# Weight splits in half-tile buffers with a longer lookahead, in an fp32 encoder trunk

## The chip, the cores and the metric

The kernel runs on one core of a Trainium2 chip. The metric is the time of one execution on the device, in microseconds, as the median of several runs. The core has five engines that work side by side, each through its own instructions in order: TensorE (PE: matmuls, and transposes as matmuls with the identity), VectorE (DVE), ScalarE (ACT), GpSimd (POOL) and SyncE (SP, which here issues loads). They wait for one another through semaphores. SBUF is the memory on the core, PSUM holds the results of matmuls in eight banks.

## The reference, cut to what matters

Two layers, 256 tokens of width 1024, everything in float32. Each layer is

```
x = x + 1/2 * SwiGLU_1(RMSNorm(x))                 # width 2816
h = RMSNorm(x)
[qA kA vA qB kB vB] = h @ W_in
oA = windowed attention (8 query heads, 2 key heads, distance bias, sink logit)
oB = differential attention (4 heads, two softmaxes), RMSNorm per head
x = x + concat(oA, oB) @ W_out
x = x + 1/2 * SwiGLU_2(RMSNorm(x))
```

with `SwiGLU(h) = (silu(h @ w_gate) * (h @ w_up)) @ w_down`, and a last RMSNorm. So there are four SwiGLU blocks, called mixers here, and two attention parts.

## The kernel before, in words

**Split operands.** PE multiplies in a float32 form of fewer bits (`float32r`). Each operand is therefore split in two: `hi` is the operand cast to that form, `lo` is the operand minus `hi`, and a product is the sum of three matmuls, hi·hi, lo·hi and hi·lo (`tokens`, lines 474 to 483; `narrow`, line 495; `prod`, line 569). Weights are split after they are loaded: ACT casts `raw` to `whi`, DVE subtracts and writes `wlo` (`emit_split`, lines 167 to 190).

**Weight tiles.** All weights are consumed in one fixed order, a list of `Step`s (`specs`, line 100 and lines 226 to 268), most of them 512 input rows by 512 columns, 1 MB. `emit_dma` (line 154) issues a load into one of six `raw` buffers, `emit_split` splits it into one of three `whi` and one of three `wlo` buffers. `weights()` (line 219) hands out the next tile i, and before that calls `ahead(i + 2)` (line 198), which emits the splits up to tile i + 2 and loads beyond it. A buffer of tile i - 1 is taken by tile i + 2, so the cast of tile i + 2 waits until PE has done its last matmul with tile i - 1. Each tile is split in two cuts of 1024 columns in all, or in four of 512 (tiles 0 to 3 and those of the attention part).

**A mixer** (`ffn`, lines 547 to 679) takes the 2816 hidden columns in five groups of 512 and a last one of 256. Group 0 uses tiles 0 to 3, group 1 tiles 4 to 9: four tiles of gate and up weights (24 matmuls each), and two of the down weights for the group before. After the first tile of a group PE transposes the hidden tile of the group before (`turn`, line 618), ACT casts it and DVE makes its `lo` part (`split`, line 485). Groups 2 and 4 (`SEVEN`, line 31) are computed by a scheme with seven products of half the size in place of eight (`by_seven`, lines 579 to 616; tiles 10 to 18 in group 2): of weights and inputs some are sums, which `make_sums` (line 304) makes on DVE during group 1 for the inputs, and for the weights `seven` (line 115) makes by DVE additions (`raw += raw`) and by loads that add into a raw buffer, issued by POOL. The order in `by_seven`: product 1 (tile 10), product 2 (tile 11), `turn` of the hidden tile, product 3 (tile 12), the first down tile (13), products 4 to 7 (tiles 14 to 17), the second down tile (18).

**Attention** (`mix`, line 723): four narrow projections, scores of four head pairs of each kind, softmax on DVE and ACT, transposes of the probabilities, products with the values, the output projection. In the first part of it the engines' order is that of the text; between `kept[0] = False` (line 796) and `kept[0] = True` (line 897) a scheduler orders the instructions of each engine. Everywhere else instructions stay in the order in which the program emits them, so a cast that waits for its buffer holds up what stands behind it on ACT, and its subtraction what stands behind it on DVE.

Tiles named `s4` (16 blocks of 4 KB per partition) hold the normed inputs, the hidden tiles, the input sums, softmax results and others; `q` (three blocks) and `v` (one) are used by attention alone.

Of the kernel before, what the change touches and what calls it, by code (L numbers as in the profile page):

```python
# [10 lines left out]
F32R = mybir.dt.float32r  # L11
AF = mybir.ActivationFunctionType
ALU = mybir.AluOpType
# [21 lines left out]
def trunk(ctx: ExitStack, tc: tile.TileContext, x, n1, g1, u1, d1, nm, w_in, sink,  # L35
# [128 lines left out]
        if s.behind is not None:  # L164
            s.behind()

    def emit_split(i):
        s = specs[i]
        kn, n, raw = s.kn, s.n, raws[s.src]
        hi = wp.tile([P, kn, n], F32R, tag="whi", bufs=N_HI, name=nm_("whi"))  # L170
        lo = wp.tile([P, kn, n], F32R, tag="wlo", bufs=N_LO, name=nm_("wlo"))
        loaded[i] = (hi, lo)
        cuts = [0, kn // 2, kn] if i > 1 and (i not in fine or kn < 4) else [kn * j // 4 for j in range(5)]
        for a, b in zip(cuts, cuts[1:]):
            if n == D:
                views = [(t[0][:, a:b, c:c + 512], t[1][:, a:b, c:c + 512], t[2][:, a:b, c:c + 512])
                         for t in [(raw, hi, lo)] for c in (0, 512)]
            elif i not in paired:
                views = [(raw[:, a:b], hi[:, a:b], lo[:, a:b])]
            else:  # L180
                views = [(raw.rearrange("p k (s c d) -> p c k s d", s=2, c=2)[:, c, a:b],
                          hi.rearrange("p k (c s d) -> p c k s d", s=2, c=2)[:, c, a:b],
                          lo.rearrange("p k (c s d) -> p c k s d", s=2, c=2)[:, c, a:b]) for c in range(2)]
            for r_, h_, l_ in views:
                act.copy(h_, r_)
                dve.tensor_tensor(l_, r_, f(h_), op=ALU.subtract)
            if i < 2:
                yield
        for k in s.free:
            raws.pop(k)  # L190

    def emit_early(i):
        yield from emit_dma(i)
        yield from emit_split(i)

    at = dict(use=0, dma=2, prep=2, split=2)

    def ahead(n):

        n = min(n, len(specs) - 1)  # L200
        while True:
            if at["split"] <= n and at["prep"] > at["split"]:
                for _ in emit_split(at["split"]):
                    pass
                at["split"] += 1
            elif at["prep"] <= min(n + 1, len(specs) - 1) and at["dma"] > at["prep"] and \
                    (specs[at["prep"]].prep is None or at["split"] >= at["prep"]):
# [65 lines left out]
    class Norm:  # L273
# [115 lines left out]
    def take_x(k):  # L389
# [8 lines left out]
        elif k == 1:  # L398
            for e in (g, u, g, u):
                next(e)  # L400
            norm.pair(2)
            ahead(2)
            norm.pair(3)
        elif k == 2:
            ahead(3)
# [65 lines left out]
            dve.tensor_scalar_mul(gsub[:, l:l + 1], gcol[:, 48 + l:49 + l], 1.0 - lam_init[l])  # L471


    def tokens(accs, xs, w, k0, ks=range(4), first=0, last=KC - 1, order=None):

        hi, lo = w
        for k, t in (order or [(k, t) for k in ks for t in range(2)]):
            kk = k0 + k
            xv = xs[kk // 2][:, kk % 2]
            xh, xl = xv[:, t * P:(t + 1) * P], xv[:, S + t * P:S + (t + 1) * P]  # L480
            pe.matmul(accs[t], lhsT=xh, rhs=hi[:, k], start=kk == first, stop=False)
            pe.matmul(accs[t], lhsT=xl, rhs=hi[:, k], start=False, stop=False)
            pe.matmul(accs[t], lhsT=xh, rhs=lo[:, k], start=False, stop=kk == (last if isinstance(last, int) else last[t]))

    def split(dst, src, scale=None):

# [7 lines left out]

    def narrow(acc, w, j, xs, kcs, first, last):

        hi, lo = w
        for i, (wk, xk) in enumerate(kcs):
            wh = hi[:, wk, j * P:(j + 1) * P]
            wl = lo[:, wk, j * P:(j + 1) * P]  # L500
# [46 lines left out]
    def ffn(norm, aside=None, before=None, final=False):  # L547
# [19 lines left out]
            return h  # L567

        def prod(xo, w):
            hi, lo = w  # L570
            acc = bank()
            for k in range(4):
                xh, xl = xo(k)
                pe.matmul(acc, lhsT=xh, rhs=hi[:, k], start=k == 0, stop=False)
                pe.matmul(acc, lhsT=xl, rhs=hi[:, k], start=False, stop=False)
                pe.matmul(acc, lhsT=xh, rhs=lo[:, k], start=False, stop=k == 3)
            return acc

        def by_seven(h, g):
# [104 lines left out]
    def ffn_end(parts, last):  # L684
# [4 lines left out]
        w = {0: weights()}  # L689

        def group(h, order, a=None, c=slice(None), first=0):
            tokens(a or accs[h], hT, [t[:, :, c] for t in w[h]], G4, first=first, last=last[h], order=order)

        def tail(h, order=BY_TOKENS, a=None, c=slice(None)):
            tokens(a or accs[h], [None] * (2 * NGRP) + hE, [t[:, h, :, c] for t in w["rest"]], 4 * NGRP, last=last[h], order=order)
# [4 lines left out]
        w["rest"] = [t.rearrange("p k (h n) -> p h k n", h=2) for t in weights()]  # L700
        w[1] = weights(LOOK - 1)
        return group, tail

    def ffn_close(parts, nxt):
# [18 lines left out]
    def mix(l, norm, nxt_norm):  # L723
# [111 lines left out]
        vB = tp.tile([P, 2, 512], F32, tag="v", bufs=1, name=nm_("v"))  # L835
        vsl = [bank() for _ in range(2)]
        for k0 in (0, 4):
            hi, lo = weights()
            for k in range(4):
                kk = k0 + k  # L840
                xv = norm.xs[kk // 2][:, kk % 2]
                for t in range(2):
                    xh, xl = xv[:, t * P:(t + 1) * P], xv[:, S + t * P:S + (t + 1) * P]
                    pe.matmul(vsl[t], lhsT=xh, rhs=hi[:, k], start=kk == 0, stop=False)
                    pe.matmul(vsl[t], lhsT=xl, rhs=hi[:, k], start=False, stop=False)
                    pe.matmul(vsl[t], lhsT=xh, rhs=lo[:, k], start=False, stop=kk == KC - 1)
# [73 lines left out]
        res = Residual(nxt_norm, accs)  # L920

        def out_part(w, k0, h, order=None):
            tokens(accs[h], oT, [t.rearrange("p k (h n) -> p h k n", h=2)[:, h] for t in w], k0, range(2), 4, 3, order)

        w = weights()
        for h in range(2):
# [112 lines left out]
```

## Time and profile before

| | before |
|---|---|
| median of 3 runs | 945.48 us (945.32 to 945.58) |
| profiled execution | 945.94 us |
| its span, first to last instruction | 944.2 us |
| DVE busy, ACT busy | 718.6 us, 538.1 us |
| PE matmuls ps<-whi,s | 699.4 us in 2252 rows |
| PE matmuls ps<-wlo,s | 438.1 us in 1126 rows |
| DVE subtractions into wlo | 433.8 us in 440 |
| ACT casts into whi | 372.0 us in 440 |
| DMA | 186.19 MB, mean 197 GB/s |
| granted TensorE clock | 0.999 |

A row of the profile names the engine, the operation, what it writes and reads by the program's names, the shapes, and how many instructions it stands for; behind a bar, or in brackets, stands the idle time of the engine just ahead of it and what ended that. All program lines show as L50, since every instruction passes one helper, so rows are told apart by their tiles: `whi` and `wlo` are split weights, `s` the s4 tiles, `tmp` and `ps` scratch and PSUM. Matmuls overlap: a row of PE lasts longer than the time until the next one may start. In the timeline the first column is the start in us from the start of the span, the second the time from the first start to the last end.

### The profile page before, as it was taken

The page shows a single profiled execution, that of the slowest core. Times are in us where ns is not written, and L with a number is a line of the kernel's source. Part 1 is how long each engine was busy: PE and PEld are TensorE (multiplying, and loading weights), DVE is VectorE, ACT ScalarE, POOL GpSimd, SP SyncE. Part 2 cuts the span into 40 slices and gives each one's busy share as a digit, 9 for nine tenths or more (in the row PEclk, how much of TensorE's full clock was granted, in tenths as well). Part 3 has the DMA queues.
Part 4 walks back from the last instruction along what each step waited for, and adds up shares of the span by engine and source line. Part 5 has one row for each costly group of instructions (what it writes and reads, how often), then busy time and mean ns, then how long its engine had stood idle before and what let it go on. Part 6 is the DMA issues. An engine that isn't in the chain of part 4 may idle for free.

```text
span 944.2 us, 12633 instructions
## 1 busy us (share of the span) xinstructions
PE 931.5 (99%) x4844; PEld 790.4 (84%) x4844; DVE 718.6 (76%) x1086; ACT 538.1 (57%) x853; POOL 40.6 (4%) x65
## 2 busy tenths in 40 slices
PE   8999999999999999999999999999999999999997
PEld 6887888899888887888888888888999888888886
DVE  5689779579856589679557995887796667995983
ACT  6647546567735547446554564656676464564653
POOL 0400000000000000000000000000000000000001
PEclk9999999999999999999999999999999999999999
DMA  9959868655424829958557498586551447497631
GB/s 336 338 140 286 246 178 303 190 179 136 134 90 144 256 92 286 293 133 306 185 179 223 97 329 243 148 300 186 170 168 56 139 174 223 104 346 241 151 118 45
DMA packets 106669, 186.19 MB, mean 197 GB/s; under 512 B 3438, under 2 KB 31152, under 8 KB 106608
## 3 DMA queue, kind: packets, MB, share of 16 engines
q1 hardware_dynamic: 96816, 167.27, 52.0%
q0 software_dynamic: 8704, 17.07, 10.5%
q10 hardware_dynamic: 1088, 1.05, 0.3%
q8 instruction: 38, 0.62, 0.3%
q14 instruction: 23, 0.19, 0.1%
HBM read 184.32 MB, written 1.05 MB: 196 GB/s over the span
## 4 chain that ended last, share of the span: by engine, by line
PE 82%; DVE 11%; ACT 4%; issue 2%; DMA 0%; ACTq 0%; POOLq 0%; POOL 0%; DVEq 0%
PE ps L50 82%; DVE wlo L50 6%; DVE tmp L50 3%; ACT whi L50 3%; DVE s L50 1%; ACT s L50 1%; DVE raw L50 0%; DMA xk<-in_x_dram 0%; ACT tmp L50 0%; DVE xk L50 0%; ACTq L50 0%; POOLq L1034 0%; POOL rf L50 0%; DVE rf L50 0%; DVEq L50 0%
## 5 line engine op out<-in xcount | busy, mean ns | idle before, releaser
L50 PE MATMUL ps<-whi,s 128*128 128x512 f32 (+1 forms) x2252 | 699.4, 391 | 2.0 <-DVE s L50 2.0
L50 DVE TENSOR_TENSOR wlo<-raw,whi 128x1024 fp32r<-128x1024 f32 (+2 forms) x440 | 433.8, 1034 | 97.7 <-ACT whi L50 95.1
L50 PEld LDWEIGHTS ps<-whi,s 128*128 128x128 f32 x2252 | 419.7, 188 | 88.4 <-DVE s L50 3.7
L50 ACT CAST whi<-raw 128x1024 fp32r<-128x1024 f32 (+2 forms) x440 | 372.0, 902 | 177.2 <-PE ps L50 117.7
L50 PE MATMUL ps<-wlo,s 128*128 128x512 f32 (+1 forms) x1126 | 438.1, 389 | 0.0
L50 PEld LDWEIGHTS ps<-wlo,s 128*128 128x128 f32 x1126 | 211.8, 188 | 43.9 <-DVE wlo L50 0.2
L50 PE MATMUL ps<-s,whi 128*128 128x256 f32 x448 | 82.7, 286 | 0.0
L50 PEld LDWEIGHTS ps<-s,whi 128*128 128x128 f32 x448 | 70.1, 192 | 1.1
L50 ACT CAST s<-ps 128x512 fp32r<-128x512 f32 x48 | 26.0, 589 | 66.0 <-PE ps L50 66.0
L50 PE MATMUL ps<-s,wlo 128*128 128x256 f32 x224 | 63.3, 283 | 0.0
L50 DVE TENSOR_TENSOR s<-ps,s 128x512 fp32r<-128x512 f32 x48 | 31.0, 685 | 41.5 <-ACT s L50 41.5
L50 PEld LDWEIGHTS ps<-s,wlo 128*128 128x128 f32 x224 | 42.9, 192 | 0.0
L50 ACT CAST s<-tmp 128x512 fp32r<-128x512 f32 (+1 forms) x22 | 13.2, 602 | 49.1 <-DVE tmp L50 49.1
L50 PE MATMUL ps<-ident,s 128*128 128x128 f32 x304 | 39.6, 273 | 0.0
L50 PEld LDWEIGHTS ps<-ident,s 128*128 128x128 f32 x304 | 35.1, 141 | 4.7
L50 POOL DMA_DIRECT2D raw<-in_ffn_w_up_dram x16 | 20.8, 1298 | 412.9 <-ACT whi L50 120.0
L50 DVE TENSOR_TENSOR raw<-raw,raw 128x1024 f32<-128x1024 f32 x32 | 37.6, 1218 | 0.0
L50 ACT ACTIVATE s<-s,negm 128x256 f32<-128x256 f32 x64 | 31.8, 501 | 7.4 <-DVE negm L50 7.4
L50 ACT ACTIVATE tmp<-ps,r 128x512 f32<-128x512 f32 (+1 forms) x32 | 19.9, 636 | 28.0 <-PE ps L50 27.9
L50 DVE SCALAR_TENSOR_TENSOR s<-ps,hr,tmp 128x512 f32<-128x512 f32 (+1 forms) x32 | 20.8, 681 | 13.4 <-PE ps L50 6.9
L50 ACT ACTIVATE s<-ps,gcol 128x256 fp32r<-128x256 f32 x48 | 19.3, 474 | 19.7 <-PE ps L50 19.7
L50 DVE SCALAR_TENSOR_TENSOR s<-ps,gcol,s 128x256 fp32r<-128x256 f32 x48 | 20.3, 477 | 13.1 <-ACT s L50 13.0
(104 smaller groups left out, 411.2 us busy)
## 6 DMA issues: line engine op xcount, KB each, us to landing
raw<-in_ffn_w_down_dram SPq DMA_DIRECT2D x44, 1024.0 KB, 5.2
raw<-in_ffn_w_gate_dram SPq DMA_DIRECT2D x39, 1024.0 KB, 6.2
raw<-in_ffn_w_up_dram SPq DMA_DIRECT2D x39, 1024.0 KB, 5.1
raw<-in_ffn_w_up_dram POOLq DMA_DIRECT2D x16, 1024.0 KB, 9.1
raw<-in_w_in_dram SPq DMA_DIRECT2D x14, 1024.0 KB, 5.1
raw<-in_ffn_w_gate_dram SPq DMA_DIRECT2D x8, 512.0 KB, 3.8
raw<-in_ffn_w_up_dram SPq DMA_DIRECT2D x8, 512.0 KB, 5.0
raw<-in_w_in_dram SPq DMA_DIRECT2D x8, 512.0 KB, 4.5
```

The costliest lines, as they stand in the source:

```text
L50: ins = issue(*a, **k)
```

## The change

A weight tile no longer has one `whi` and one `wlo` buffer of full size. It has two halves, each with a `hi` and a `lo` buffer of half size, and all of them come from one pool of 14 (tag `w`): seven halves. Halves are cut along the input rows for the tiles of 512 by 512, along the columns for those of 256 or 1024 columns. `weights()` for tile i emits the splits up to half 2i + 6, that is the first half of tile i + 3, and the first use of the tile's second half emits half 2i + 7 (class `Split`, method `part`). A call can ask for `less` halves, and `held` keeps the second half from emitting any: that is used for product 2 of `by_seven` (`weights(2, True)`) and for the first two tiles of attention. The fourth input sum now stands, in the emitted order, behind the split of tile 11 and the addition for tile 12.

Loads may be issued up to 10 tiles ahead instead of 8; there are still six raw buffers. There are 14 s4 blocks instead of 16; the four input sums go to the three `q` blocks and the `v` block. A half is split in one cut of 1024 columns in all, or in two of 512 for tiles 0 to 3 and those of attention; the two tiles whose columns are paired lose their cuts of 256.

PE issues the same matmuls. Their order is the same but for the scheduled part of attention, where a few scores and transposes change places.

```diff
-LOOK, AHEAD = 2, 8
-N_RAW, N_HI, N_LO = 6, 3, 3
-N_S4 = 16
+AHEAD = 10
+N_RAW, N_W = 6, 14
+N_S4 = 14
...
-    def emit_split(i):
+    class Split:
+        def __init__(self, i):
+            self.i, self.n, self.parts, self.held = i, specs[i].n, [], False
+
+        def part(self, k, c=slice(None), h=None):
+            if h is None:
+                h, k = divmod(k, 2)
+            if h and not self.held:
+                self.held = True
+                ahead(2 * self.i + 1 + HALVES)
+            return [t[:, k, c] for t in self.parts[h]]
+
+    def emit_split(i, j):
         s = specs[i]
...
+        shape = (P, 8, P) if s.n == 256 else (P, 2, 512)
+        hi, lo = [wp.tile(list(shape), F32R, tag="w", bufs=N_W, name=nm_("w")) for _ in range(2)]
+        loaded[i].parts.append((hi, lo))
...
+        m = shape[1] // 2 if i < 2 or i in fine else shape[1]
+        for a in range(0, shape[1], m):
+            r_, h_, l_ = [t[:, a:a + m] for t in (raw, hi, lo)]
+            act.copy(h_, r_)
+            dve.tensor_tensor(l_, r_, f(h_), op=ALU.subtract)
             if i < 2:
                 yield
-        for k in s.free:
-            raws.pop(k)
+        if j == 1:
+            for k in s.free:
+                raws.pop(k)
...
+    HALVES = N_W // 2 - 1
+    at = dict(use=0, dma=2, prep=2, split=4)
...
-    def weights(look=LOOK):
+    def weights(less=0, held=False):
         i = at["use"]
         at["use"] += 1
         if i > 1:
-            ahead(i + look)
-        return loaded.pop(i)
+            ahead(2 * i + HALVES - less)
+        w = loaded[i]
+        w.held = held
+        return w
...
-                sm = blk().rearrange("p a (c s) -> p (a c) s", c=2)
+                tag, n = ("q", 3) if len(self.sm) < 3 else ("v", 1)
+                sm = tp.tile([P, 2, 512], F32R, tag=tag, bufs=n, name=nm_(tag)).rearrange("p a (c s) -> p (a c) s", c=2)
...
-            p7 = prod(norm.summed(2), weights())
+            p7 = prod(norm.summed(2), weights(2, True))
...
-        ws = (weights(), weights(LOOK - 1))
+        ws = (weights(), weights(2))
...
-        ahead(at["use"] + LOOK - 1)
+        ahead(2 * at["use"] - 2 + HALVES)
...
-        s0, s1 = first_groups(norm, (weights(), weights(LOOK - 1)))
+        s0, s1 = first_groups(norm, (weights(held=True), weights(2, True)))
```

More of the change, by code (lines that the diff above doesn't have):

```diff
@@ L165, in emit_dma @@
             s.behind()
-    def emit_split(i):
-        s = specs[i]
[L169 to L186, printed above, removed]
+    class Split:
[8 more added lines that the diff above has]
+            return [t[:, k, c] for t in self.parts[h]]
@@ new lines, in emit_split @@
+    def emit_split(i, j):
+        s = specs[i]
+        raw = raws[s.src]
+        if j == 0:
+            loaded[i] = Split(i)
+        shape = (P, 8, P) if s.n == 256 else (P, 2, 512)
+        hi, lo = [wp.tile(list(shape), F32R, tag="w", bufs=N_W, name=nm_("w")) for _ in range(2)]
+        loaded[i].parts.append((hi, lo))
+        if s.n == D:
+            raw = raw[:, :, j * 512:(j + 1) * 512]
+        elif i in paired:
+            raw = raw.rearrange("p k (s c d) -> p c k s d", s=2, c=2)[:, j]
+            hi, lo = [t.rearrange("p k (s d) -> p k s d", s=2) for t in (hi, lo)]
+        elif s.n == 256:
+            raw = raw[:, :, j * P:(j + 1) * P]
+        else:
+            raw = raw[:, 2 * j:2 * j + 2]
+        m = shape[1] // 2 if i < 2 or i in fine else shape[1]
[3 more added lines that the diff above has]
+            dve.tensor_tensor(l_, r_, f(h_), op=ALU.subtract)
@@ L187, in emit_split @@
             if i < 2:
                 yield
-        for k in s.free:
-            raws.pop(k)
+        if j == 1:
+            for k in s.free:
+                raws.pop(k)
     def emit_early(i):
         yield from emit_dma(i)
-        yield from emit_split(i)
-    at = dict(use=0, dma=2, prep=2, split=2)
+        for j in range(2):
+            yield from emit_split(i, j)
+    HALVES = N_W // 2 - 1
+    at = dict(use=0, dma=2, prep=2, split=4)
     def ahead(n):
-        n = min(n, len(specs) - 1)
+        n = min(n, 2 * len(specs) - 1)
@@ L201, in ahead @@
         while True:
-            if at["split"] <= n and at["prep"] > at["split"]:
-                for _ in emit_split(at["split"]):
+            if at["split"] <= n and at["prep"] > at["split"] // 2:
+                for _ in emit_split(*divmod(at["split"], 2)):
                     pass
                 at["split"] += 1
-            elif at["prep"] <= min(n + 1, len(specs) - 1) and at["dma"] > at["prep"] and \
-                    (specs[at["prep"]].prep is None or at["split"] >= at["prep"]):
+            elif at["prep"] <= min(n // 2 + 1, len(specs) - 1) and at["dma"] > at["prep"] and \
+                    (specs[at["prep"]].prep is None or at["split"] >= 2 * at["prep"]):
@@ L401, in take_x @@
             norm.pair(2)
-            ahead(2)
+            ahead(5)
             norm.pair(3)
         elif k == 2:
-            ahead(3)
+            ahead(7)
             for t in range(2):
@@ L471, in attention_constants, with tokens @@
             dve.tensor_scalar_mul(gsub[:, l:l + 1], gcol[:, 48 + l:49 + l], 1.0 - lam_init[l])
-    def tokens(accs, xs, w, k0, ks=range(4), first=0, last=KC - 1, order=None):
-        hi, lo = w
+    def tokens(accs, xs, w, k0, ks=range(4), first=0, last=KC - 1, order=None, cols=slice(None), h=None):
         for k, t in (order or [(k, t) for k in ks for t in range(2)]):
             kk = k0 + k
+            hi, lo = w.part(k, cols, h)
             xv = xs[kk // 2][:, kk % 2]
             xh, xl = xv[:, t * P:(t + 1) * P], xv[:, S + t * P:S + (t + 1) * P]
-            pe.matmul(accs[t], lhsT=xh, rhs=hi[:, k], start=kk == first, stop=False)
-            pe.matmul(accs[t], lhsT=xl, rhs=hi[:, k], start=False, stop=False)
-            pe.matmul(accs[t], lhsT=xh, rhs=lo[:, k], start=False, stop=kk == (last if isinstance(last, int) else last[t]))
+            pe.matmul(accs[t], lhsT=xh, rhs=hi, start=kk == first, stop=False)
+            pe.matmul(accs[t], lhsT=xl, rhs=hi, start=False, stop=False)
+            pe.matmul(accs[t], lhsT=xh, rhs=lo, start=False, stop=kk == (last if isinstance(last, int) else last[t]))
     def split(dst, src, scale=None):
@@ L495, in narrow @@
     def narrow(acc, w, j, xs, kcs, first, last):
-        hi, lo = w
         for i, (wk, xk) in enumerate(kcs):
-            wh = hi[:, wk, j * P:(j + 1) * P]
-            wl = lo[:, wk, j * P:(j + 1) * P]
+            wh, wl = w.part(wk, h=j)
             xv = xs[xk // 2][:, xk % 2]
@@ L569, in prod @@
         def prod(xo, w):
-            hi, lo = w
             acc = bank()
             for k in range(4):
+                hi, lo = w.part(k)
                 xh, xl = xo(k)
-                pe.matmul(acc, lhsT=xh, rhs=hi[:, k], start=k == 0, stop=False)
-                pe.matmul(acc, lhsT=xl, rhs=hi[:, k], start=False, stop=False)
-                pe.matmul(acc, lhsT=xh, rhs=lo[:, k], start=False, stop=k == 3)
+                pe.matmul(acc, lhsT=xh, rhs=hi, start=k == 0, stop=False)
+                pe.matmul(acc, lhsT=xl, rhs=hi, start=False, stop=False)
+                pe.matmul(acc, lhsT=xh, rhs=lo, start=False, stop=k == 3)
             return acc
@@ L691, in group @@
         def group(h, order, a=None, c=slice(None), first=0):
-            tokens(a or accs[h], hT, [t[:, :, c] for t in w[h]], G4, first=first, last=last[h], order=order)
+            tokens(a or accs[h], hT, w[h], G4, first=first, last=last[h], order=order, cols=c)
         def tail(h, order=BY_TOKENS, a=None, c=slice(None)):
-            tokens(a or accs[h], [None] * (2 * NGRP) + hE, [t[:, h, :, c] for t in w["rest"]], 4 * NGRP, last=last[h], order=order)
+            tokens(a or accs[h], [None] * (2 * NGRP) + hE, w["rest"], 4 * NGRP, last=last[h], order=order, cols=c, h=h)
         group(0, [(k, t) for k in range(3) for t in range(2)])
@@ L699, in ffn_end @@
         group(0, [(3, t) for t in range(2)])
-        w["rest"] = [t.rearrange("p k (h n) -> p h k n", h=2) for t in weights()]
-        w[1] = weights(LOOK - 1)
+        w["rest"] = weights()
+        w[1] = weights(2)
         return group, tail
@@ L837, in mix @@
         for k0 in (0, 4):
-            hi, lo = weights()
+            w = weights()
             for k in range(4):
                 kk = k0 + k
+                hi, lo = w.part(k)
                 xv = norm.xs[kk // 2][:, kk % 2]
@@ L843, in mix @@
                     xh, xl = xv[:, t * P:(t + 1) * P], xv[:, S + t * P:S + (t + 1) * P]
-                    pe.matmul(vsl[t], lhsT=xh, rhs=hi[:, k], start=kk == 0, stop=False)
-                    pe.matmul(vsl[t], lhsT=xl, rhs=hi[:, k], start=False, stop=False)
-                    pe.matmul(vsl[t], lhsT=xh, rhs=lo[:, k], start=False, stop=kk == KC - 1)
+                    pe.matmul(vsl[t], lhsT=xh, rhs=hi, start=kk == 0, stop=False)
+                    pe.matmul(vsl[t], lhsT=xl, rhs=hi, start=False, stop=False)
+                    pe.matmul(vsl[t], lhsT=xh, rhs=lo, start=False, stop=kk == KC - 1)
             if k0 == 0:
@@ L922, in out_part @@
         def out_part(w, k0, h, order=None):
-            tokens(accs[h], oT, [t.rearrange("p k (h n) -> p h k n", h=2)[:, h] for t in w], k0, range(2), 4, 3, order)
+            tokens(accs[h], oT, w, k0, range(2), 4, 3, order, h=h)
         w = weights()
```

## The prediction

> **What bounds the kernel now.** I read the head of the page first, then the waits by engine, then the chain of waits in order of time, and last the timeline around what the chain points to.
>
> ```profile
> span 944.2 us, 12633 instructions
> ...
> PE 931.5 (99%) x4844; PEld 790.4 (84%) x4844; DVE 718.6 (76%) x1086; ACT 538.1 (57%) x853; POOL 40.6 (4%) x65
> ```
> ```profile
> ACT whi L50 <- PE ps L50: 117.7, 46, 4.8
> ...
> PE ps L50 <- DMA grow<-in_ffn_norm_dram: 3.2, 1, 3.2
> ...
> PE ps L50 <- DVE s L50: 2.0, 4, 0.5
> ```
>
> TensorE (PE) is busy for 99% of the span, and the change issues the same 4748 matmuls, transposes included, as before: only their waits and a few places can change. Two waits of PE have a name: 3.2 us for the first load, and four waits for VectorE (DVE), 2.0 us in all. The chain of waits shows where the four are: each time PE takes over from a DVE instruction on a tile s.
>
> ```profile
> 73.96 0.69 DVE s L50
> 74.70 245.82 PE ps L50 x1415
> ...
> 357.23 0.70 DVE s L50
> 357.97 144.22 PE ps L50 x659
> ...
> 538.88 0.70 DVE s L50
> 539.62 245.52 PE ps L50 x1414
> ...
> 821.83 0.70 DVE s L50
> 822.57 110.72 PE ps L50 x501
> ```
>
> These are the four channel mixers (two per layer), at the same point of each: group 2, the first of the two groups made by seven products, `down(hT, g - 1, 0, ...)` in line 596, which needs the lower part of the turned hidden tile that `turn` splits. The timeline of the first one:
>
> ```profile
> 73.58 0.39 PE L50 MATMUL ps<-wlo,s 128*128 128x512 f32 x1
> ...
> 73.81 0.39 PE L50 MATMUL ps<-whi,s 128*128 128x512 f32 x1
> 73.96 1.28 DVE L50 TENSOR_TENSOR s<-ps,s 128x512 fp32r<-128x512 f32 x2
> ...
> 74.70 0.50 PE L50 MATMUL ps<-whi,s 128*128 128x512 f32 x1 [0.51 <-DVE s L50]
> ...
> 75.04 0.40 PE L50 MATMUL ps<-wlo,s 128*128 128x512 f32 x1
> ```
>
> Matmuls start 0.23 us apart (73.58, 73.81). The second one of the down product should have started at 74.04; it starts at 74.70, 0.66 us late, and the next follows after 0.34 instead of 0.23. So one place costs 0.66 + 0.11 = 0.77 us, and four cost 3.1 us. That is more than the 2.0 us of the waits view, since a matmul's row lasts 0.39 us while the next could start after 0.23: the idle column starts to count too late.
> By the Trainium skill, "Perfetto Trace Analysis", section "Summary: the profiler window per engine type", the window of a TensorE row ends at an estimated end. The rows agree (0.39 us long, 0.23 us apart); by the idle column the four would be worth 2.0 us, by the starts 3.1. I take the starts.
>
> **The change, part by part.** I number the weight tiles of a mixer from 0: group 0 uses 0 to 3, group 1 uses 4 to 9, group 2 uses 10 to 18. ScalarE (ACT) casts each to whi, DVE makes the rest wlo.
>
> (1) More lookahead. Before, three whole tiles fit, and tile i + 2 is cast once PE is done with tile i - 1. After, seven halves fit, and half n is cast once PE is done with half n - 7: the first half of tile i + 3 at the start of tile i, the second in the middle of it. What that does is seen where DVE was idle before group 2:
>
> ```profile
> 31.17 2.01 ACT L50 CAST whi<-raw 128x1024 fp32r<-128x1024 f32 x2 [1.41 <-PE ps L50]
> 37.29 1.07 ACT L50 CAST s<-ps 128x512 fp32r<-128x512 f32 x2 [4.11 <-PE ps L50]
> 38.25 2.00 ACT L50 CAST whi<-raw 128x1024 fp32r<-128x1024 f32 x2
> ```
> ```profile
> 33.58 1.22 DVE L50 TENSOR_TENSOR wlo<-raw,whi 128x1024 fp32r<-128x1024 f32 x1
> 37.90 1.29 DVE L50 TENSOR_TENSOR s<-ps,s 128x512 fp32r<-128x512 f32 x2 [3.10 <-ACT s L50]
> 39.34 2.36 DVE L50 TENSOR_TENSOR wlo<-raw,whi 128x1024 fp32r<-128x1024 f32 x2
> ```
> ```profile
> 36.65 1.03 PE L50 MATMUL ps<-ident,s 128*128 128x128 f32 x8
> 37.44 0.48 PE L50 MATMUL ps<-whi,s 128*128 128x512 f32 x1
> ```
>
> DVE finishes tile 6 at 34.8, then has nothing for 3.10 us: tile 7 may not be cast before PE is done with tile 4 (36.65), and the program has the turned tile ahead of it. From 37.90 to 73.96 DVE never rests except for ACT's casts, and arrives 0.7 us late. In the changed program tile 7 stands before the turned tile: its halves are free when PE is done with tile 3 and half of tile 4 (about 31 and 34), its 2 x 1.14 us fit into the idle 3.10 us, and the turned tile is still split at 37.90. Next comes tile 8: first half as soon as ACT has it (39.34 as before, until 40.5), second half when PE is halfway through tile 5, 37.44 + 12 x 0.23 = 40.2, plus a cast of 1.05 = 41.3, plus 1.14 = 42.4. Before, DVE had tile 7 done at 41.62; now it has tile 8 done at 42.4. One tile of 2.28 us is ahead, 0.8 us is lost on the way: **1.4 to 1.5 us gained**.
>
> (2) From there to the point of the stall DVE has the same list in both programs: tiles up to 13, the four sums of `make_sums`, two halves of `raw += raw`, two results; only the fourth sum moves behind that addition. The last tiles before the stall were
>
> ```profile
> 69.20 4.85 DVE L50 TENSOR_TENSOR wlo<-raw,whi 128x1024 fp32r<-128x1024 f32 x4
> ```
>
> tiles 12 and 13, then the turned tile at 73.96. With 1.4 us gained it is split at 72.5 to 73.2, and PE asks for it at 74.04: the stall goes, with 0.8 us to spare. The "held" second product keeps it so. Without it the longer lookahead would put half of tile 14 (1.2 us) ahead of the turned tile; with it, tile 13 is the last, as before. What is late next? The third product wants tile 12 at 71.0: it is done by 69.20 + 2.4 - 1.4, about 70.2, first half 69.1. Tile 14 follows the turned tile, then the addition for tile 15, tiles 15, 16, 17, each 2.3 us: ready at about 76, 81, 84 and 87, against the fourth to seventh product at 79, 82, 85 and 87 (down 24 x 0.23 = 5.5 us from 73.8, then 12 x 0.23 each). Those margins are 0.7 to 3 us; DVE's order moves two evictions of products behind tile 15, which the bank of the sixth product waits for, 3 us before it is needed. So no new stall, but little spare. Gain: 4 x 0.77 = **3.1 us**. Bounds: 0, if nothing is gained on DVE, and 3.1.
>
> (3) Loads. SP's and GpSimd's queues issue the same loads in the same order (one pair swaps in the last mixer); each waits for a raw buffer that an earlier split frees, so all come as early or earlier. The tightest is the accumulating load on which tile 11 waits:
>
> ```profile
> raw<-in_ffn_w_up_dram POOLq DMA_DIRECT2D x16, 1024.0 KB, 9.1
> ```
> ```profile
> 44.28 1.38 POOL L50 DMA_DIRECT2D raw<-in_ffn_w_up_dram  x1 [6.20 <-DVE tmp L50]
> ```
>
> Issued at 44.3 and landed near 53 to 55, it is wanted at about 58: cost nothing, covered by DVE's sums; without that cover up to 5 us, once.
>
> (4) Fewer small instructions: 32 casts and 32 subtractions of 256 columns become 8 and 8 of 1024. ACT and DVE do not bound those places; nothing. In the first mixer ACT now casts tile 4 before the sums of squares, so the scale and the first gated result come about 2 us later; that is covered, since its turn starts at 36.65 and the result is there by 34.5.
>
> (5) The attention part, order of PE. The scheduler puts the first softmax scores of the windowed heads in one stretch of 24 instead of 4 and 20:
>
> ```profile
> 236.49 0.50 PE L50 MATMUL ps<-s,q 64*128 64x256 f32 x4
> 236.92 1.09 PE L50 MATMUL ps<-ident,s 128*128 128x128 f32 x8
> 237.77 0.48 PE L50 MATMUL ps<-whi,s 128*128 128x512 f32 x1
> ...
> 240.24 1.46 PE L50 MATMUL ps<-s,q 64*128 64x256 f32 x20
> 241.62 0.50 PE L50 MATMUL ps<-whi,s 128*128 128x512 f32 x1
> ...
> 245.92 1.70 PE L50 MATMUL ps<-s,q 64*128 64x256 f32 x24
> 247.55 0.55 PE L50 MATMUL ps<-ident,s 128*128 128x128 f32 x3
> ```
>
> From start to start, 4 and 20 take 0.43 + 1.38 = 1.81 us, an unbroken 24 takes 1.63: 0.18 less. The wide matmuls (10 from 237.77, 2.47 us; 18 from 241.62, 4.30 us) cost 0.20 and 0.16 more than 0.23 each would, and there is one such stretch fewer: 0.2 less. So 0.38 per layer, **0.8 us** for two. Bounds: 0 and 1.0. The fewer s4 blocks (14 instead of 16) take no wait here that I can find: each block's earlier reader stands well ahead on PE, since the sums now use the idle q and v buffers.
>
> Sum on the profiled execution: 944.2 - 3.1 - 0.8 = 940.3 us of span. Around the span lie 945.94 - 944.2 = 1.7 us, so 942.0; the profiled execution is 0.46 us above the median 945.48, hence **941.6**.
>
> **The rivals.**
> The stall stays (944.7). DVE may not get ahead: if the second halves, which wait for the middle of a PE tile, cost at every tile what they cost at tile 8 (0.8 us), the 2.28 us are gone after three tiles. For it: the margin is 0.8 us. Against: after tile 8 DVE is behind PE's releases, not ahead of them (tile 9 is freed at 43 to 46 and wanted at 46). Then only part 5 is left: 945.48 - 0.8 = 944.7.
> By the Trainium skill, "Perfetto Trace Analysis", section "Optimization Strategy", a gap that keeps its size on the busy engine can mean that the next tile has no space. Here the row names DVE for PE's gap, and PE for ACT's (117.7 us): by that rule the space decides and 3.1 us go; by PE's row alone DVE's work decides and they stay.
>
> The stall moves (944.7). Tiles 14 and 15 are not cast during the second product, so products 5 to 7 could wait instead, with margins of 0.7 to 1.5 us; the same 0.77 us four times.
>
> Slower, 949.4. In the attention part casts for the output projection now stand on ACT ahead of the exponentials of the last two head pairs, and ACT keeps its order. If such a cast waits until PE has left the second value tile (near 253.98) instead of the first, eight exponentials of 0.5 us follow late.
>
> ```profile
> 253.43 0.50 ACT L50 ACTIVATE s<-s,negm 128x256 f32<-128x256 f32 x1
> ...
> 253.93 0.29 ACT L50 ACTIVATE es<-es 128x4 f32<-128x4 f32 x2
> ```
>
> Now the last ends at 253.93 and PE needs it after 16 transposes, near 255.7: 1.8 us of slack. Starting at 254 + 1.2 for the casts they would end at 259.6, 3.9 us late, in both layers: 941.6 + 7.8. It makes the kernel slower than now from 2.0 us of lateness per layer. Against it: half n - 7 of that cast belongs to the first value tile, which PE leaves at about 244.6, and then the last exponential ends before 252.
>
> **How the numbers follow.** Forecast 0.72 (its own range 940.6 to 942.8); stall stays 0.12; stall moves 0.08; slower 0.08. The range goes from 940.6 (part 5 a little better, part of the start-up gap gone) to 944.9, which holds both cases of 944.7. A measurement of this kernel can tell 0.2%, 1.9 us: faster is below 943.6. The forecast with some of the halfway cases gives 0.75 for faster, the two 944.7 cases most of 0.17 for the same, 0.08 for slower.
>
> **What would show it.** The waits view should have no wait of PE for DVE on an s tile, and the chain should no longer leave PE near 37, 320, 502 and 785. DVE's subtraction on the first turned tile of group 2 should end before PE's second down matmul, by 0.5 to 1 us. In attention the scores should stand as 4, 20, 24, 24 and 24. I am wrong if a PE start gap over 0.5 us stands in group 2 behind a w tile (the stall moved), behind an s tile (DVE got nothing ahead), or in the transposes near 254 (the exponentials came late).

## The result, and the profile after

| | before | after |
|---|---|---|
| median | 945.58 us (5 runs on this chip, 945.32 to 945.89) | 942.07 us (5 runs, 941.68 to 944.21) |
| profiled execution, its span | 945.94 us, 944.2 us | 942.07 us, 940.3 us |
| DVE busy, ACT busy | 718.6 us, 538.1 us | 722.2 us, 539.1 us |

The ratio of the times is 0.9967, with a 95% interval of 0.9952 to 0.9981: about 0.33% faster. Forecast were 941.6 us and a span of 940.3 us. The number came out, and so did the way it was to come about; the experiments show that one of its two parts could also have been had by a much smaller edit.

The waits of PE in the changed kernel, with total, count and longest:

```profile
PE ps L50 <- DMA grow<-in_ffn_norm_dram: 3.4, 1, 3.4
```

The view has no wait of PE's matmuls for DVE on an s tile any more, and PE's share of the chain that ended last is now 96%: between 5.4 and 929 us it leaves PE only once, from 81.6 to 107.7 us, and at none of the four places. The same place in group 2 of the first mixer, in the timeline of the changed kernel (start, length, engine):

```profile
67.31 4.63 DVE L50 TENSOR_TENSOR w<-raw,w 128x1024 fp32r<-128x1024 f32 x4 [0.26 <-PE ps L50]
...
70.03 0.57 ACT L50 COPY tmp<-ps 128x512 f32<-128x512 f32 x1
70.50 1.08 ACT L50 CAST s<-ps 128x512 fp32r<-128x512 f32 x2
...
70.66 3.01 PE L50 MATMUL ps<-w,q 128*128 128x512 f32 x12
...
71.86 1.28 DVE L50 TENSOR_TENSOR s<-ps,s 128x512 fp32r<-128x512 f32 x2
...
73.06 2.35 DVE L50 TENSOR_TENSOR w<-raw,w 128x1024 fp32r<-128x1024 f32 x2
...
73.50 1.75 PE L50 MATMUL ps<-w,s 128*128 128x512 f32 x7
```

The first line is tiles 12 and 13, two halves each: the work on DVE ahead of the turned tile is that of before. DVE splits the turned tile from 71.86, where it came at 73.96 before. Its first half (0.69 us) is done at 72.55, and PE wants it at 73.50 + 0.23 = 73.73: 1.18 us to spare. Before, it was done at 74.65 and wanted at 74.04, 0.61 us late. So DVE has gained 1.8 us on PE. Keep an eye on the second and fourth lines: ACT's copy of product 1 ends at 70.60, and PE's third product, which waits for the bank that the copy frees, starts at 70.66.

One thing is new. In group 3 of the first mixer the constants of the attention part stand ahead of the turned tile on DVE:

```profile
100.66 0.19 DVE L50 COPY gcol<-ps 128x34 f32<-128x34 f32 x1
100.76 0.42 DVE L50 CAST distA<-dist_i 128x512 f32<-128x512 int32 x1
...
104.64 2.36 DVE L50 TENSOR_TENSOR w<-raw,w 128x1024 fp32r<-128x1024 f32 x2 [0.41 <-ACT w L50]
...
106.92 1.28 DVE L50 TENSOR_TENSOR s<-ps,s 128x512 fp32r<-128x512 f32 x2
...
107.65 1.46 PEld L50 LDWEIGHTS ps<-w,s 128*128 128x128 f32 x7 [0.48 <-DVE s L50]
```

A whole tile is now cast between the constants and the turned tile, which comes late by some 0.3 us.

To compare kernels I measure PE's way from start to start of the same instructions. What the load of the first tiles leaves to chance ends within the first 100 instructions of PE (the 101st starts at 27.4 to 28.6 us in these profiles), so I take the rest of the way from there, and four stretches of it: group 2 of the first mixer, group 3 of the first mixer, and the stretches around the two attention parts.

| profiled kernel | rest of PE's way | group 2 | group 3 | attention 1 | attention 2 |
|---|---|---|---|---|---|
| before | 909.06 us | 29.36 | 40.05 | 110.71 | 155.15 |
| after | 905.50 us | 28.57 | 40.41 | 110.36 | 154.76 |

Group 2 gains 0.79 us, and its three later counterparts 0.80, 0.82 and 0.77 (66.99 to 66.19, 105.07 to 104.25, 66.97 to 66.20): 3.2 us for the four stalls. Group 3 loses 0.36. Attention gains 0.35 and 0.39. That is 3.2 - 0.36 + 0.74 = 3.56 us, all of 909.06 - 905.50. The remaining 0.3 us between the spans (3.9 us) lies in the first 28 us, where the kernel before and the run with the hold alone (below), whose programs are the same there, also differ by 0.35 us.

### The profile page after: what moved, and what is told of

Read it like the earlier page. It is cut to its first block, busy times and chain, and to the rows that moved or that the text cites. A ratio compares the mean times of both kernels' runs of the same rounds, so it can differ in the third digit from the quotient of the medians.

```text
span 940.3 us, 12909 instructions
## 1 busy us (share of the span) xinstructions
PE 929.6 (99%) x4844; PEld 790.5 (84%) x4844; DVE 722.2 (77%) x1062; ACT 539.1 (57%) x829; POOL 41.3 (4%) x65
## 4 chain that ended last, share of the span: by engine, by line
PE 96%; DVE 1%; issue 1%; ACT 1%; DMA 0%; ACTq 0%; POOLq 0%; POOL 0%; DVEq 0%
PE ps L50 96%; ACT w L50 1%; DVE w L50 0%; DMA xk<-in_x_dram 0%; DVE s L50 0%; DVE tmp L50 0%; DVE distA L50 0%; ACT tmp L50 0%; DVE distB L50 0%; DVE xk L50 0%; ACTq L50 0%; POOLq L1057 0%; POOL rf L50 0%; DVE lsum L50 0%; DVE rf L50 0%
## 5 line engine op out<-in xcount | busy, mean ns | idle before, releaser
L50 PE MATMUL ps<-w,s 128*128 128x512 f32 (+1 forms) x2994 | 691.0, 390 | 0.1
L50 PEld LDWEIGHTS ps<-w,s 128*128 128x128 f32 x2994 | 557.7, 188 | 114.5 <-DVE s L50 0.7
L50 DVE TENSOR_TENSOR w<-raw,w 128x1024 fp32r<-128x1024 f32 (+1 forms) x416 | 440.8, 1089 | 113.8 <-ACT w L50 110.4
L50 ACT CAST w<-raw 128x1024 fp32r<-128x1024 f32 (+1 forms) x416 | 373.3, 941 | 173.1 <-PE ps L50 126.0
L50 PE MATMUL ps<-s,w 128*128 128x256 f32 x672 | 84.0, 285 | 0.0
L50 PEld LDWEIGHTS ps<-s,w 128*128 128x128 f32 x672 | 81.7, 191 | 1.1
L50 PE MATMUL ps<-w,q 128*128 128x512 f32 x288 | 70.1, 392 | 0.0
L50 PEld LDWEIGHTS ps<-w,q 128*128 128x128 f32 x288 | 53.5, 188 | 10.7
L50 DVE TENSOR_TENSOR tmp<-tmp,s 128x256 f32<-128x256 f32 x56 | 23.4, 425 | 1.6
L50 PE MATMUL ps<-w,v 128*128 128x512 f32 x96 | 23.1, 389 | 0.0
```

The lines of the kernel that those rows point to most:

```text
L50: ins = issue(*a, **k)
```

## The experiments

Theory of the prediction: the longer lookahead gets DVE 1.4 us ahead, which ends the stall; the hold in product 2 only keeps it so. Rival A: the lookahead does it alone. Rival B: the hold does it alone, by the order on DVE. In "lookahead or not" by "hold or not", the kernel before and the changed one are two of four corners; the first two runs are the others. But the hold is not the same thing in the two kernels. With the longer lookahead tile 13 is split during product 1 already, so the hold keeps only tile 14 and what follows it behind the turned tile, and the work ahead of the turned tile stays that of before. In the kernel before, the hold takes tile 13 out of that work. The times of the kernel before on the chips of these runs were 945.3, 945.6, 945.49 and 945.44 us.

**The lookahead without the hold.**

```diff
-            p7 = prod(norm.summed(2), weights(2, True))
+            p7 = prod(norm.summed(2), weights())
```

> The changed kernel without the hold: product 2 casts ahead again, seven halves as changed. Theory of the prediction (the longer lookahead gets DVE ahead, the hold keeps it there): both halves of tile 14, 2 x 1.15 us of DVE, now stand ahead of the turned tile; the spare time there is about 1.2 us in the changed kernel's trace, so PE is late by some 1.1 us at each of the four places, with the slower next start 1.2: 942.1 + 4.8 = 946.9 us, with four waits of PE for DVE on an s tile. Rival A (the lookahead alone is enough, the hold is ornament): 942.1 us, no such wait.

966.41 us (962.45 to 967.95), ratio 1.0215 (1.0194 to 1.0237). Rival A falls: with more work put ahead of the turned tile the lookahead does not help. The loss is far larger than the theory's. Timeline of this kernel in group 2:

```profile
68.37 5.76 DVE L50 TENSOR_TENSOR w<-raw,w 128x1024 fp32r<-128x1024 f32 x5
...
73.45 0.39 PE L50 MATMUL ps<-w,s 128*128 128x512 f32 x1
74.05 2.35 DVE L50 TENSOR_TENSOR raw<-raw,raw 128x1024 f32<-128x1024 f32 x2
...
76.32 1.28 DVE L50 TENSOR_TENSOR s<-ps,s 128x512 fp32r<-128x512 f32 x2
...
77.06 2.23 PE L50 MATMUL ps<-w,s 128*128 128x512 f32 x7 [3.21 <-DVE s L50]
```

I had forgotten the addition for tile 15, which comes with the casts of tile 14: 2.28 + 2.35 = 4.6 us ahead of the turned tile, less 1.18 us of spare time, makes 3.4 us of stall. And what follows the stall is slow. Busy times and the granted clock (the number behind POOL) of this kernel by stretch:

```profile
72.00:77.00 5.00, 1.84 (x9) 1.16 (x7) 5.00 (x6) 2.92 (x5) 0.00 (x0) 1.00 0.68 220
77.00:81.00 4.00, 3.94 (x12) 3.14 (x13) 3.96 (x6) 1.86 (x3) 0.00 (x0) 0.68 0.81 264
81.00:84.00 3.00, 3.00 (x12) 2.44 (x12) 2.46 (x3) 0.70 (x1) 0.00 (x0) 0.86 0.96 311
```

For some 4 us the clock is granted in part (0.68), and eight matmuls start 0.427 us apart in place of 0.227: 1.75 us more. One place costs 5.15 us, four cost 20.6. The turned tile of group 4 has the same list ahead of it and comes 0.48 us late, four times.

**The hold without the lookahead.**

```diff
 # the kernel before: whole tiles, three of each
-            p7 = prod(norm.summed(2), weights())
+            p7 = prod(norm.summed(2), weights(LOOK - 1))
```

> The kernel before with the hold as its only change: product 2 of the seven casts nothing, so tile 13 is split behind the turned tile. Whole tiles, three of each, as before. Theory of the prediction (DVE has to gain on PE, and only the longer lookahead gives it that): the same list of work on DVE is as late as before, the turned tile comes in time but tile 13 takes its place as the late one, 945.5 us, 944.5 at best. Rival B (the order alone is enough): the turned tile is split 2.4 us sooner, near 71.6 to 72.9, tile 13 from 72.9, its first half done near 74.1, just ahead of PE's first use of it at 74.3: all four stalls go, 945.5 - 3.1 = 942.4 us, without a deeper lookahead.

942.79 us (942.41 to 943.61), ratio 0.9973 (0.9961 to 0.9984): the rival's time. The small edit takes all four stalls, so it is not true that only the longer lookahead can. It does not show that the hold took them in the changed kernel, where tile 13 still stands ahead of the turned tile. Its timeline:

```profile
68.83 2.36 DVE L50 TENSOR_TENSOR wlo<-raw,whi 128x1024 fp32r<-128x1024 f32 x2
...
71.11 1.28 DVE L50 TENSOR_TENSOR s<-ps,s 128x512 fp32r<-128x512 f32 x2
...
72.52 3.50 DVE L50 TENSOR_TENSOR wlo<-raw,whi 128x1024 fp32r<-128x1024 f32 x3
...
73.45 0.62 PE L50 MATMUL ps<-whi,s 128*128 128x512 f32 x2
73.80 0.19 PEld L50 LDWEIGHTS ps<-wlo,s 128*128 128x128 f32 x1 [0.16 <-DVE wlo L50]
```

The list of work on DVE is as late as before, but tile 13 stands behind the turned tile, and PE wants its first half a matmul later than the turned tile and its second half 2.7 us later still. The turned tile comes at 71.11, earlier than in the changed kernel; tile 13 is just in time, with 0.16 us of wait for a weight load that delays the next matmul by less than 0.02 us. Group 2 takes 28.61 us here, 28.57 in the changed kernel. Group 3 has no new wait: 40.05 us. Attention is that of before (110.71 and 155.19).

**More depth than the change gives, in whole tiles.** The hold, four whole tiles (`LOOK = 3`), the sums in `q` and `v`, `N_S4 = 12`.

> The kernel before with the hold and with four whole tiles in place of three (one whole tile more of lookahead, more than the change gives), the input sums in the q and v blocks, and 12 s4 blocks to make room. No halves. The order of PE's score stretches in attention is that of before. Theory after the first runs (in group 2 the order of the turned tile decides, depth brings nothing of its own): as with the hold alone, 942.8 us, or up to 0.4 more, since the deeper list also brings the wait at group 3 of the first mixer. Rival (the longer lookahead has a gain of its own): 942.1 us or less without any change in attention.

943.01 us (942.31 to 943.51), ratio 0.9971 (0.9961 to 0.9982); group 2 28.57 us, group 3 40.05, attention 110.69 and 155.13. The time is that of the hold alone. The order on DVE is not:

```profile
68.00 4.63 DVE L50 TENSOR_TENSOR wlo<-raw,whi 128x1024 fp32r<-128x1024 f32 x4 [0.26 <-PE ps L50]
72.55 1.28 DVE L50 TENSOR_TENSOR s<-ps,s 128x512 fp32r<-128x512 f32 x2
...
74.18 0.62 PE L50 MATMUL ps<-whi,s 128*128 128x512 f32 x2
```

Tiles 12 and 13 both stand ahead of the turned tile, as in the kernel before, and yet its first half (0.69 us) is done at 73.24, 1.17 us before PE wants it (74.18 + 0.23). At the three later places the margin is 1.9 us. So the theory put here, that depth brings nothing of its own, falls: the longer lookahead ends the stalls without a shorter list on DVE, and without halves. Either way alone is enough, and having both brings nothing more at the four places: the rest of PE's way is 905.77 us against 906.39 with the hold alone, 0.6 us in steps of some 0.05 us elsewhere in the kernel, which the times do not show.

**Six halves, the space of before.** `N_W = 12` in the changed kernel.

> The changed kernel with six halves in place of seven: the space for split weights is that of before. Theory of the prediction (seven halves are needed): only the first half of tile 7 fits into DVE's idle stretch, about half of the gain on DVE is lost, and tiles come 1.1 us later: stalls of 0.3 to 0.8 us come back in group 2, 943.5 to 945 us. Rival B (the order of the turned tile alone): the second half of tile 13 now also stands behind the turned tile, so no stall comes back there: 942.1 us.

943.85 us (943.25 to 944.41), ratio 0.9984 (0.9975 to 0.9993). The time lies in the theory's range, but not for its reason. PE's waits in this kernel, and its timeline:

```profile
PE ps L50 <- ACT tmp L50: 1.1, 4, 0.3
```
```profile
66.93 3.15 ACT L50 CAST w<-raw 128x1024 fp32r<-128x1024 f32 x3 [2.50 <-DVE raw L50]
...
69.98 0.57 ACT L50 COPY tmp<-ps 128x512 f32<-128x512 f32 x1
...
70.60 3.04 PE L50 MATMUL ps<-w,q 128*128 128x512 f32 x12 [0.27 <-ACT tmp L50]
```

The turned tile is in time (71.43). PE's third product waits for ACT's copy of product 1, behind three casts that wait for DVE's addition. From start to start it costs 0.55 us, four times: 2.2 us. The wait in group 3 of the first mixer is not there (0.3 us less), which leaves the 1.9 us by which PE's way is longer than in the changed kernel (907.42 and 905.50 us). That is the narrow margin seen above, used up.

**One half more, and one tile more.** Between the hold and none: product 2 casts the first half of tile 14 (`weights(0, True)`); or both halves, without the addition.

> The changed kernel in which product 2 casts one half more ahead (the first half of tile 14, one cast and one subtraction of 1.14 us), and no addition: this is what the prediction feared without the hold. Theory: the turned tile's subtraction comes 1.14 us later, against 1.18 us of spare time in the changed kernel's trace: 942.1 us, at most 0.2 us of waits per place. Rival (the spare time is smaller than it looks): 0.3 to 0.8 us per place, 943.3 to 945.3 us. If all of the loss without the hold came with this half, it would be near 966.

> The changed kernel in which product 2 casts both halves of tile 14 ahead of the turned tile, but not the addition for tile 15 that came with them in the run without the hold. Theory (the loss without the hold is DVE's work ahead of the turned tile less 1.18 us of spare time, plus eight matmuls at half pace after a long wait): the turned tile is 2 x 1.14 us later, PE waits some 1.1 us at each of four places. If a wait of 1.1 us is too short for the half pace, as the 0.66 us of the kernel before were: 942.3 + 4 x 1.2 = 947.1 us. If it is long enough, as 2.07 and 3.4 us were: 1.6 us more at each, 953.5 us. Rival (the addition or something else in that run made the loss): 942.3 us.

One half: 942.49 us (942.15 to 942.91). PE's matmuls have no wait at the turned tile, only the next one starts 0.1 us late: the turned tile now has 0.07 us to spare, so the 1.18 us were real. One tile: 947.53 us (946.59 to 948.69), ratio 1.0022 (1.0013 to 1.0032), with these waits of PE:

```profile
PE ps L50 <- DVE s L50: 3.9, 4, 1.0
```

From start to start 1.13 us are lost each time, and the next start adds 0.11; matmuls keep their pace of 0.23 us afterwards. So the loss without the hold is counted, per place: 1.13 us of wait with tile 14, 2.25 more with the addition (3.38), and 1.75 for the half pace, 5.13 of the 5.15 us. Over all these runs the margin of the turned tile follows the list on DVE: 1.18 us in the changed kernel, 0.07 with a half more, -1.08 (late) with a tile more, -3.32 with the addition too.

**The constants behind the turned tile.** `aside()` moved from ahead of group 3 to behind its `turn`.

> The changed kernel with the constants of the attention part made behind the turned tile of group 3 of the first mixer instead of ahead of it. The changed kernel's trace has a new wait there (PE starts 0.33 us late near 107.7, for DVE's split of the turned tile, with 3.4 us of constants ahead of it on DVE). Theory: the wait goes, 942.07 - 0.33 = 941.7 us, since DVE idles 1.5 us at each of the next tiles. Rival: the 3.4 us then hold up the next split tile, and PE waits for that instead: 942.1 us or more.

945.1 us (944.29 to 946.12), ratio 0.9996 (0.9987 to 1.0005): 3 us lost, neither case. Timeline and stretches:

```profile
100.23 1.03 PE L50 MATMUL ps<-ident,s 128*128 128x128 f32 x8
...
102.44 1.28 DVE L50 TENSOR_TENSOR s<-ps,s 128x512 fp32r<-128x512 f32 x2
...
103.17 0.25 PE L50 MATMUL ps<-ident,grow 34*128 34x34 f32 x1 [1.91 <-DVE s L50]
```
```profile
103.00:108.00 5.00, 4.83 (x14) 3.82 (x15) 4.19 (x14) 1.55 (x4) 0.83 (x1) 0.66 1.05 353
```

The constants contain an instruction of PE, the transpose of the gains, and that needs a bank. Behind `turn` the next bank is one that the turned tile holds until DVE has split it, so PE stands still for 2.07 us, and again runs at half pace for eight matmuls (1.7 us more).

**The constants in two parts.** PE's transpose and its copy stay, DVE's work on distances and lambdas goes behind the turned tile.

> The changed kernel with the attention constants in two parts: PE's transpose of the gains and its copy stay ahead of group 3 of the first mixer, the 2.9 us of DVE work on distances and lambdas go behind the turned tile. Theory (the run with all constants behind the turned tile lost 3 us because PE's transpose of the gains then waited for a bank that the turned tile held, 2.07 us and then eight slow matmuls, not because of DVE's work): no wait of PE there, 942.07 - 0.33 = 941.7 us. Rival (the 2.9 us of DVE work hold up the next split tile wherever they stand): 942.1 us or more, with a wait of PE for DVE on a w tile after 107 us.

942.55 us (941.74 to 942.88), ratio 0.9966 (0.9953 to 0.9978). Group 3 takes 40.05 us, so the new wait is gone and the rival falls. But group 2 takes 29.48 us in this profile, by a wait for the copy of product 1 (0.86 us from start to start):

```profile
PE ps L50 <- ACT tmp L50: 0.6, 1, 0.6
```

**The changed kernel again, and one with product 1 held too.** The second is the kernel with split constants, and

```diff
-            p1 = prod(norm.quarter(0, 0), weights())
+            p1 = prod(norm.quarter(0, 0), weights(held=True))
```

> The changed kernel once more, unchanged, on the chip of the run beside it, so that differences of a few tenths of a us can be compared. 942.1 us; its slower executions (944.2 was seen once) should show PE waiting for ACT's copy of product 1 if the late load is their cause.

> The changed kernel with the constants split as in the run before (PE's part ahead of group 3, DVE's behind the turned tile), and product 1 of the seven held as well, so that the second half of tile 13 is cast behind the turned tile. Theory (in the changed kernel PE's third product has only about 0.06 us to spare for ACT's copy of product 1, which frees its bank and stands behind the cast of that half; a load 1.7 us later cost 0.78 us there in the run with split constants): the copy comes 0.95 us sooner, no wait of PE for ACT's copy in any profile, 941.7 us. Rival (the half of tile 13 then comes late for the down product): a wait of PE for a w tile near 76 us, four times, 942.5 us or more.

The changed kernel: 942.63 us (942.25 to 942.84), ratio 0.9968 (0.9955 to 0.998). Its profile has the same wait, and shows where it begins:

```profile
58.89 2.00 ACT L50 CAST w<-raw 128x1024 fp32r<-128x1024 f32 x2 [1.55 <-DMA raw<-in_ffn_w_up_dram]
...
66.75 3.89 ACT L50 CAST w<-raw 128x1024 fp32r<-128x1024 f32 x4
70.55 0.57 ACT L50 COPY tmp<-ps 128x512 f32<-128x512 f32 x1
...
71.17 3.01 PE L50 MATMUL ps<-w,q 128*128 128x512 f32 x12 [0.43 <-ACT tmp L50]
```

ACT waits for the accumulating load until 58.89; in the first profile of the changed kernel it cast at 57.60. Tile 11, the addition, the fourth sum and the casts of tiles 12 and 13 follow one another from there, and the copy comes last: 0.68 us lost in group 2 (29.25 us).

With product 1 held the second half of tile 13 is out of that row:

```profile
58.72 2.00 ACT L50 CAST w<-raw 128x1024 fp32r<-128x1024 f32 x2 [1.38 <-DMA raw<-in_ffn_w_up_dram]
...
66.58 2.95 ACT L50 CAST w<-raw 128x1024 fp32r<-128x1024 f32 x3
69.44 0.57 ACT L50 COPY tmp<-ps 128x512 f32<-128x512 f32 x1
```

The load is as late, the copy stands 1.1 us sooner, PE waits for nothing, and the rest of PE's way is 905.24 us, the shortest of all (changed kernel 905.50 and 906.26). Its median is 942.39 us (941.75 to 942.62), ratio 0.9965 (0.9952 to 0.9979). It beats the kernel before; that it beats the changed one (942.63 beside it) the times cannot tell.

**Attention: more stretches.** The score matmuls of the changed kernel emitted under `urgent()`.

> The changed kernel with the score matmuls at high priority for the scheduler, which breaks them into seven stretches per layer (4, 20, 3, 21, 4, 20, 24) in place of five (4, 20, 24, 24, 24). The matmuls are the same. Theory (every further stretch costs 0.34 to 0.38 us): two more per layer, four in all, 1.4 to 1.5 us: 943.5 us. Rival (the 0.7 us in attention came from something else): 942.1 us.

944.21 us (943.71 to 945.33), ratio 0.9987 (0.9978 to 0.9996). Attention takes 111.29 and 155.70 us, 0.93 and 0.94 more than in the changed kernel, for two stretches more in each layer: 0.47 us per stretch. The rival falls: breaking up the scores costs time. The price is a third over the 0.34 to 0.38 us of the theory, and the run also moves stretches to other places; what it is in a stretch that costs was not taken apart.

## Why the prediction was right, and where it was wrong

- *What bounds the kernel, 0.77 us per place by the starts:* right, 0.77 to 0.82 per place. By the idle column it would have been 0.5. (The count of 4748 matmuls is not that of the profile, which has 4844 rows of PE in both kernels.)
- *Step 1, DVE gains 1.4 to 1.5 us before group 2:* right, and a little low. In the changed kernel DVE does tile 7 from 34.6 to 37.0 us, the turned tile from 37.6, tile 8 until 42.2 (forecast 42.4). At the turned tile of group 2 the gain on PE is 1.8 us, from 0.61 late to 1.18 early.
- *Step 2, "with 1.4 us gained ... the stall goes", the hold "keeps it so":* right. With the same list ahead of the turned tile the stalls are there at the old depth (the kernel before) and gone at the greater one (the changed kernel, and the run with four whole tiles). Without the hold the list grows by 4.6 us and the gain is lost, so in this change both parts are needed. The forecast had two gaps. "Half of tile 14 (1.2 us)" was too little for what the hold keeps away: both halves and the addition behind them. And it asked only how late DVE is, and not for what: tile 13 is not wanted before the turned tile, so putting it behind, without any depth, would have taken the stalls as well.
- *"No new stall, but little spare":* true of products 4 to 7, where none waits. Not listed were the third product's bank (0.06 us to spare, 0.7 and 0.9 us lost in two profiles) and group 3 of the first mixer (0.36 us lost): I followed DVE's casts and not ACT's copy, and stopped at the end of group 2.
- *Step 3, loads "all come as early or earlier", cost nothing:* wrong at the one load I called tightest. The group of DMA issues between 40 and 50 us, with the size and the us to landing, first before, then after:

```profile
raw<-in_ffn_w_gate_dram SPq DMA_DIRECT2D x1, 1024.0 KB, 7.3
raw<-in_ffn_w_up_dram POOLq DMA_DIRECT2D x1, 1024.0 KB, 11.0
raw<-in_ffn_w_up_dram SPq DMA_DIRECT2D x1, 1024.0 KB, 9.1
```
```profile
raw<-in_ffn_w_up_dram SPq DMA_DIRECT2D x1, 1024.0 KB, 13.6
raw<-in_ffn_w_up_dram POOLq DMA_DIRECT2D x1, 1024.0 KB, 13.3
raw<-in_ffn_w_down_dram SPq DMA_DIRECT2D x1, 1024.0 KB, 10.7
```

  Casting sooner frees raw buffers sooner: a load of one megabyte that was issued at 48.2 us before is issued at 42.3, ahead of the accumulating load (44.3 and 44.2). That one needs 13.3 us in place of 11.0 and lands at 57.5; in the kernel's second profile it needs 14.5, and ACT waits for it until 58.9. With the hold alone, in the old depth, it needs 10.9. My bound, "up to 5 us, once", was the right kind of bound; taking 0 left out the 0.7 us lost in the second profile. The two medians, 942.07 and 942.63, differ by about as much, but only one execution of each is profiled.
- *Step 4, fewer small instructions, nothing:* ACT and DVE issue 24 fewer each, as forecast; no run shows what they are worth alone.
- *Step 5, attention, 0.38 us per layer:* right, 0.35 and 0.39, with scores in stretches of 4, 20, 24, 24 and 24 as forecast. (One of its terms is a little large: 2.47 us less ten times 0.23 is 0.17, not 0.20.)
- *The rivals:* no wait of a matmul for an s tile stayed, nothing moved to products 5 to 7, and the exponentials came in time. (The sum of the slower rival is 0.4 us too long per layer: eight exponentials of 0.5 us from 255.2 end at 259.2.)
- *The sum:* 3.1 + 0.8 forecast; 3.2 + 0.74 - 0.36 measured, and 0.3 us by chance in the first 28 us. That the span came out to the tenth is luck: the 0.36 us lost in group 3, which the forecast did not have, and the 0.3 us at the start cancelled.

## What to carry to other kernels

Where engines keep the program's order, look at each instruction ahead of the late one and ask when its own reader wants it: moving one tile behind the turned tile took all four stalls, without space or depth. Longer lookahead took them too, but it is not free: it puts work ahead of urgent work on the same engine, and loads ahead of urgent loads, so it needs a place where it stops. When a step is moved, list what it takes on every engine, banks included.

## What the runs showed of the hardware

A long wait can cost PE more than its length. After waits of 2.07 us and 3.4 us (start to start, beyond the usual pace) the granted clock is 0.66 over the next 5 us and 0.68 over the next 4, and about eight 128x512 matmuls start 0.427 us apart, some 1.7 us in all; after 1.13 us and 0.67 us, four times each, they keep 0.227. The wait of 2.07 us stands directly behind eight transposes (0.9 us) and ahead of a ninth, the others between matmuls, so these runs do not give the length from which a wait costs more. The Trainium skill, "TensorE: Matmul & The Clock Gate", section "What's actually happening", has the clock fall to half after an idle window of about 3.4 us. The half pace agrees (0.427 us against 0.227), and the wait of 3.4 us fits; the one of 2.07 us is shorter, and whether the transposes ahead of it explain that is open.
